# Loading each dense phase's input block in four transfers instead of one

## The chip, the cores and the metric

The kernel runs on one core of a Trainium2 chip. The metric is the time of one execution in microseconds (us), as the device measures it; lower is better. A core has five engines that run side by side, each in the order of its own queue: TensorE (PE; matmuls, with weight loads as PEld), VectorE (DVE), ScalarE (ACT), GpSimd (POOL) and SyncE (SP), which here does nothing but issue transfers between the main memory and the on-chip memory.

## The reference

One layer of a hybrid encoder for a prompt of 2048 tokens and a sample of 32 tokens, in float32, model width 1024, feed-forward width 4096. Cut to what matters:

```python
def trunk_layer(x, mem_k, mem_v, k_past, v_past, shift_prev, wkv0, lw, table):
    z = rmsnorm(x, lw['norm_mix_g']) @ lw['w_in']
    q, k, v, zr = jnp.split(z, ...)
    a_out, k_buf, v_buf = window_attention(q, k, v, k_past, v_past, lw['attn_sink'], table)
    r_out, shift_new, S = rwkv7_mixer(zr, shift_prev, wkv0, lw)        # recurrent over the tokens
    x = x + jnp.concatenate([a_out, r_out], axis=-1) @ lw['w_out']
    x = x + memory_cross_attention(rmsnorm(x, lw['norm_cross_g']), mem_k, mem_v, lw)
    hm = rmsnorm(x, lw['norm_mlp_g'])
    x = x + jnp.square(jax.nn.relu(hm @ lw['w_up'])) @ lw['w_down']
    return x, k_buf, v_buf, shift_new, S
```

The memory's keys and values come from `rmsnorm(mem) @ w_mk` and `rmsnorm(mem) @ w_mv` (256 tokens). A last RMSNorm follows. The outputs are both token blocks and the updated caches and states.

## The kernel before

All activations are kept transposed: 128 rows (partitions) by chunks of the width by tokens. A width of 1024 is eight chunks of 128. The 2080 tokens are worked on in four groups (0 to 3) of 544, 512, 512 and 512 tokens, each in two blocks of 272 or 256.

There are two stages. The first, up to about 1770 us of the trace, holds:

- the dense phases, all made by `prep` (an input block is loaded and split) and `dense` (loop over weight units, and for each over the two blocks): Y and Z (w_in, input x, 8 chunks), M (the memory's keys and values, 8 chunks), O (w_out, input mscr, 8 chunks), C (w_cq, input x2scr, 8 chunks), D (w_co, input cscr, 4 chunks). Z uses the blocks that Y loaded;
- the RWKV tiles R (17 of them, recurrent one after the other, many small matmuls), the window attention tiles A and the cross attention jobs X, and L, which loads blocks for the second stage.

The second stage is the feed-forward part, six blocks of 352 or 320 tokens against 32 weight units up and down, with its own loads.

Float32 accuracy is had from three matmuls for each chunk (`mm3`, lines 230 to 237): the input block is split into a high part xh, rounded by ScalarE, and a low part xl, the rest, by VectorE or GpSimd; weights are split likewise into w_h and w_l (`load_w`, lines 252 to 259: two transfers w_raw of 256 KB for each unit, ScalarE for w_h, then GpSimd or VectorE for w_l). The three products xh w_h, xl w_h and xh w_l are lines 234, 235 and 236. A unit on a block of eight chunks is 24 matmuls that add up in one PSUM tile ps_z, of which there are two; VectorE evacuates it (zo, zoq).

`prep` (lines 264 to 297) loads the block into the tile xb, of which there is one (line 277). Where the phase has a norm (Y, M, C), each chunk gives one xh (ScalarE) and one xl (VectorE), lines 294 to 296, and later, in `rms`, one square on ScalarE, summed on GpSimd, from which the norm comes that the evacuation multiplies by. Where it has none (O, D), each pair of chunks gives one xh and one xl (lines 289 to 292). The next block's load has to wait until the last reader of xb is through. In the listing of the profile, helpers record ScalarE's work at line 66 and VectorE's and GpSimd's at lines 69 and 72.

What sets the order: all of it is written in the order of PLAN (line 35), and a planner at build time then orders each engine's queue from a simulated timeline (line 37), by priorities that the code sets (`setp`, lines 205 to 210): RWKV's serial parts first, the dense matmuls of `mm3` last. At run time each engine follows its queue in order, and a wait holds what stands behind it. Every load of xb, w_raw and the rest stands in SyncE's queue; only a few stores are issued by ScalarE.

The very first block (Y0's first) already comes in four transfers of two chunks (lines 278 to 280, `pe` is true there alone). Y0's second block goes into three tiles of its own (lines 265 to 272).

Of the kernel before, what the change touches and what calls it, by code (L numbers as in the profile page):

```python
# [50 lines left out]
def hymba_step_kernel(  # L51
# [9 lines left out]
    V, G, S, T, Q = nc.vector, nc.gpsimd, nc.scalar, nc.tensor, nc.sync  # L61
# [36 lines left out]
    def pc(key, i, n=1):  # L98
        return par[:, PG[key] + i:PG[key] + i + n]
# [72 lines left out]
    def split(xt, h, l, eng=None):  # L172
        act(h, xt)
        tt(l, xt, h.bitcast(F32), SUB, eng)
# [18 lines left out]
    def rms(pool, xk, n, tag, pe=False, bufs=1):  # L193
        acc, ps = sumsq(pool, xk, n, tag, pe, bufs)
        act(acc, ps, AF.Ln, bias=eps_t, scale=1.0 / D)
        act(acc, acc, AF.Exp, scale=-0.5)
        return acc

    def gsplit(xk, h, l, g):
        act(h, xk, scale=g)  # L200
        stt(l, xk, g, h.bitcast(F32), MUL, SUB)
# [62 lines left out]
    def prep(src, nb, gkey, nk=KC, pe=False, alt=False):  # L264
        if alt:
            xa = [rp.tile([P, 1024], F32, tag=t, name="xa", bufs=BKB if t == "bk" else 1) for t in ("bk", "wa", "lt")]
            xs_ = []
            for j, t in enumerate(xa):
                w = min(3, nk - 3 * j)
                v = t[:, 0:w * nb].rearrange("p (a b) -> p a b", a=w)  # L270
                Q.dma_start(v, src[:, 3 * j:3 * j + w])
                xs_ += [v[:, i] for i in range(w)]

            def xk(k):
                return xs_[k]
        else:
            xb = zp.tile([P, KC, NH], F32, tag="xb", name="xb", bufs=1)
            if pe:
                for k in range(0, nk, 2):
                    Q.dma_start(xb[:, k:k + 2, 0:nb], src[:, k:k + 2])  # L280
            else:
                Q.dma_start(xb[:, 0:nk, 0:nb], src)

            def xk(k):
                return xb[:, k, 0:nb]
        xh = [zp.tile([P, XS, NH], F32R, tag="xh", name="xh", bufs=XB) for k in range(0, nk, XS)]
        xl = [zp.tile([P, XS, NH], F32R, tag="xl", name="xl", bufs=XB) for k in range(0, nk, XS)]
        if gkey is None:
            for k in range(0, nk, 2):
                a, b = divmod(k, XS)  # L290
                split(xb[:, k:k + 2, 0:nb], xh[a][:, b:b + 2, 0:nb], xl[a][:, b:b + 2, 0:nb],
                      ENG[E6] if k % 4 else V)
            return xh, xl, None
        for k in range(nk):
            a, b = divmod(k, XS)
            gsplit(xk(k), xh[a][:, b, 0:nb], xl[a][:, b, 0:nb], pc(gkey, k))
        return xh, xl, lambda: rms(zp, xk, nb, "zt", pe, 3)
# [23 lines left out]
    def zphase(g, units):  # L321
# [3 lines left out]
        if g not in zst:  # L325
            def xprep(b0, nb):
                return prep(xT3[:, :, o + b0:o + b0 + nb], nb, "mix", pe=(g == 0), alt=(g == 0 and b0 > 0))

            zst[g] = ([(lambda b=b: xprep(*b)) if g == 0 and b[0] else xprep(*b) for b in blks], [None] * 2)
# [52 lines left out]
    def memphase():  # L382
        lab("mem")
        xs = [prep(memT.rearrange("(k p) t -> p k t", p=P), NMEM, "mem")]

        def evk(h, bi, b0, nb, ps, r):
            zo = zp.tile([P, NH], F32, tag="zo", name="zok", bufs=3)
            tt(zo[:, 0:nb], ps[:, 0:nb], r, MUL)
            Q.dma_start(kxs[:, h], zo[:, 0:nb])
            Q.dma_start(pmkT[:, h], zo[:, 0:nb])  # L390

        def evv(h, bi, b0, nb, ps, r):
            zo = zp.tile([P, NH], F32, tag="zo", name="zov", bufs=3)
            tt(zo[:, 0:nb], ps[:, 0:nb], r, MUL)
            pt = pmm("pvx")
            for m in range(2):
                T.transpose(pt[:, m * P:(m + 1) * P], zo[:, m * P:(m + 1) * P], ident)
            zv_ = zp.tile([P, NH], F32, tag="zo", name="zovt", bufs=3)
            act(zv_[:, 0:nb], pt[:, 0:nb])
            zv3 = zv_[:, 0:nb].rearrange("p (a b) -> p a b", a=2)  # L400
            Q.dma_start(vxs[:, :, h * P:(h + 1) * P], zv3)
            Q.dma_start(pmv[:, :, h * P:(h + 1) * P], zv3)

        dense(wmk, range(4), xs, [(0, NMEM)], evk)
        dense(wmv, range(4), xs, [(0, NMEM)], evv)

    def ophase(g):
        lab(f"O{g}")
        o, n = GROUPS[g]
        blks = halves_of(g)  # L410
        xs = [prep(mscr[g][:, :, b0:b0 + nb], nb, None) for b0, nb in blks]

        def evac(m, bi, b0, nb, ps, r):
            xr = zp.tile([P, NH], F32, tag="zm", name="xres", bufs=3)
            Q.dma_start(xr[:, 0:nb], xT3[:, m, o + b0:o + b0 + nb])
            zo = zp.tile([P, NH], F32, tag="zo", name="zo2", bufs=3)
            tt(zo[:, 0:nb], ps[:, 0:nb], xr[:, 0:nb], ADD)
            Q.dma_start(x2scr[g][:, m, b0:b0 + nb], zo[:, 0:nb])

        dense(wout, range(8), xs, blks, evac)  # L420
# [507 lines left out]
    for it in PLAN.split():  # L928
        k = it[0]
# [242 lines left out]
```

## Time and profile before

| | |
|---|---|
| median of 3 runs | 3261.2 us (3257.1 to 3262.8) |
| the profiled execution | 3264.6 us |
| its span, first to last instruction | 3262.8 us |
| mean granted TensorE clock | 0.960 |
| loads of xb in one transfer | 31 (23 of eight chunks, 8 of four) |

How to read the rows below: times are us from the start of the span, unless they are marked ns. PE is a matmul, PEld a weight load, SPq a transfer being issued by SyncE. `out<-in` are the program's names of tiles, `x8` a count. In the timeline a row gives the start, the time from there to the end, the engine, the line, the operation, and in brackets how long the engine stood idle before it and what ended that. In the table of stretches PEclk is the granted clock of TensorE as a share of full speed. "DMA to landing" is the time from the start of an issue to the landing of its data.

### The profile page before, as it was taken

What the parts mean: (1) busy time and instruction counts of PE and PEld (TensorE: products, weight loads), DVE (VectorE), ACT (ScalarE), POOL (GpSimd) and SP (SyncE); (2) the same over time, 40 slices, a digit from 0 to 9 for tenths busy, and PEclk for the clock granted to TensorE, in tenths of its full rate; (3) what the DMA queues carried; (4) which work ended last, traced back from release to release, by engine and by line L of the source; (5) the groups of instructions that cost most, each with busy time, mean ns of one, the idle gap of its engine ahead of it and who ended that gap; (6) DMA issues with size and microseconds to landing.
All of it is one profiled execution on the core that took longest, in us unless ns stands there. A gap on an engine that the chain in (4) does not pass through costs nothing.

```text
span 3262.8 us, 64716 instructions
## 1 busy us (share of the span) xinstructions
PE 3037.4 (93%) x25605; PEld 2850.0 (87%) x25605; DVE 1896.0 (58%) x4482; ACT 1247.0 (38%) x2824; POOL 1012.4 (31%) x1017
## 2 busy tenths in 40 slices
PE   8989888998879988898978999999999999999998
PEld 7877776877768977778978999999999999999998
DVE  4588777887777567853334544444445644444446
ACT  5355454444455444445443322222224322222223
POOL 3443354323354343425554410111013511011111
PEclk9989888999989999999989999999999999999999
DMA  5443343334344454446765211111113111111112
GB/s 167 134 115 108 104 130 108 108 96 122 109 122 123 135 150 120 130 129 195 242 214 178 68 51 41 46 46 52 40 46 115 66 44 52 40 52 52 46 46 91
DMA packets 336752, 328.95 MB, mean 101 GB/s; under 512 B 82320, under 2 KB 256064, under 8 KB 336448
## 3 DMA queue, kind: packets, MB, share of 16 engines
q1 hardware_dynamic: 306640, 311.83, 31.0%
q10 hardware_dynamic: 29808, 12.98, 1.6%
q8 instruction: 201, 3.29, 0.4%
q14 instruction: 103, 0.84, 0.1%
HBM read 252.59 MB, written 72.39 MB: 100 GB/s over the span
## 4 chain that ended last, share of the span: by engine, by line
PE 53%; DMA 8%; DVE 7%; ACT 3%; POOL 2%; issue 2%; SPq 1%; DVEq 0%; ACTq 0%; POOLq 0%
PE ps_up L236 7%; PE ps_dn L1002 7%; PE ps_dn L1004 7%; PE ps_dn L1003 7%; PE ps_up L234 7%; PE ps_up L235 7%; PE ps_z L234 2%; PE ps_z L236 2%; PE ps_z L235 2%; DMA xb<-x2scr 2%; DMA lt<-lscr 1%; ACT xh L66 1%; DVE z L69 1%; DVE prd L69 1%; DVE xt L69 1%
## 5 line engine op out<-in xcount | busy, mean ns | idle before, releaser
L234 PE MATMUL ps_z<-xh,w_h 128*128 128x256 f32 (+1 forms) x2368 | 722.8, 305 | 98.3 <-DVE zo L69 41.1
L236 PE MATMUL ps_z<-xh,w_l 128*128 128x256 f32 (+1 forms) x2368 | 715.0, 302 | 0.8 <-POOL w_l L69 0.8
L235 PE MATMUL ps_z<-xl,w_h 128*128 128x256 f32 (+1 forms) x2368 | 714.0, 302 | 1.4 <-DVE xl L72 0.8
L66 ACT ACTIVATE w_h<-w_raw 128x512 fp32r<-128x512 f32 x576 | 344.5, 626 | 777.7 <-PE ps_up L235 258.5
L69 DVE TENSOR_TENSOR x<-ps_dn,x 128x352 f32<-128x352 f32 (+1 forms) x768 | 389.6, 516 | 365.0 <-PE ps_dn L1004 364.5
L234 PEld LDWEIGHTS ps_z<-xh,w_h 128*128 128x128 f32 x2368 | 478.0, 202 | 124.1 <-DVE zo L69 34.2
L69 POOL TENSOR_TENSOR w_l<-w_raw,w_h 128x512 fp32r<-128x512 f32 x300 | 394.9, 1332 | 580.6 <-ACT w_h L66 481.0
L69 POOL TENSOR_TENSOR rl<-rl 128x352 f32<-128x352 f32 (+1 forms) x192 | 161.1, 840 | 1138.4 <-ACT uh L66 1136.4
L1002 PE MATMUL ps_dn<-uh,w_h 128*128 128x352 f32 (+1 forms) x1536 | 492.9, 321 | 4.2 <-DVE x L69 3.1
L236 PE MATMUL ps_up<-fh,w_l 128*128 128x352 f32 (+1 forms) x1536 | 495.4, 323 | 1.2 <-DVE w_l L69 1.2
L1003 PE MATMUL ps_dn<-ul,w_h 128*128 128x352 f32 (+1 forms) x1536 | 491.1, 320 | 5.0 <-DVE ul L69 5.0
L234 PE MATMUL ps_up<-fh,w_h 128*128 128x352 f32 (+1 forms) x1536 | 493.2, 321 | 0.5 <-DVE zo L69 0.5
L235 PEld LDWEIGHTS ps_z<-xl,w_h 128*128 128x128 f32 x2368 | 478.3, 202 | 15.9 <-issue 9.6
L236 PEld LDWEIGHTS ps_z<-xh,w_l 128*128 128x128 f32 x2368 | 478.0, 202 | 15.2 <-issue 10.4
L235 PE MATMUL ps_up<-fl,w_h 128*128 128x352 f32 (+1 forms) x1536 | 491.1, 320 | 0.1
L1004 PE MATMUL ps_dn<-uh,w_l 128*128 128x352 f32 (+1 forms) x1536 | 490.8, 320 | 0.0
L69 DVE TENSOR_TENSOR w_l<-w_raw,w_h 128x512 fp32r<-128x512 f32 x276 | 197.7, 735 | 222.0 <-ACT w_h L66 221.5
L1003 PEld LDWEIGHTS ps_dn<-ul,w_h 128*128 128x128 f32 x1536 | 289.9, 189 | 5.6 <-DVE ul L69 5.3
L1002 PEld LDWEIGHTS ps_dn<-uh,w_h 128*128 128x128 f32 x1536 | 288.6, 188 | 6.5 <-DVE x L69 3.0
L236 PEld LDWEIGHTS ps_up<-fh,w_l 128*128 128x128 f32 x1536 | 288.4, 188 | 1.7 <-DVE w_l L69 1.5
L1004 PEld LDWEIGHTS ps_dn<-uh,w_l 128*128 128x128 f32 x1536 | 289.2, 188 | 0.2
L234 PEld LDWEIGHTS ps_up<-fh,w_h 128*128 128x128 f32 x1536 | 288.3, 188 | 1.3 <-DVE zo L69 0.7
(245 smaller groups left out, 4478.5 us busy)
## 6 DMA issues: line engine op xcount, KB each, us to landing
w_raw<-in_win SPq DMA_DIRECT2D x160, 256.0 KB, 2.9
w_raw<-in_wup SPq DMA_DIRECT2D x136, 256.0 KB, 2.6
w_raw<-in_wdn SPq DMA_DIRECT2D x136, 256.0 KB, 2.6
w_raw<-in_wout SPq DMA_DIRECT2D x64, 256.0 KB, 3.2
zrw<-zo SPq DMA_DIRECT2D x84, 128.0 KB, 2.1
lt<-lscr SPq DMA_DIRECT2D x34, 244.0 KB, 3.8
zin<-zrw SPq DMA_DIRECT2D x16, 512.0 KB, 3.8
w_raw<-in_wcq SPq DMA_DIRECT2D x32, 256.0 KB, 3.4
```

Of the source, the lines that this page charges most:

```text
L66: S.activation(out, in_, func, **kw)
L69: (eng or V).tensor_tensor(out, a, b, op=op)
L234: T.matmul(ps, lhsT=a, rhs=c, start=(k == 0), stop=False)
L235: T.matmul(ps, lhsT=a, rhs=d, start=False, stop=False)
L236: T.matmul(ps, lhsT=b, rhs=c, start=False, stop=(k == nk - 1))
L1002: T.matmul(ps[:, 0:n], lhsT=wh[:, ms], rhs=us[i][0], start=(i == 0), stop=False)
L1003: T.matmul(ps[:, 0:n], lhsT=wh[:, ms], rhs=us[i][1], start=False, stop=False)
L1004: T.matmul(ps[:, 0:n], lhsT=wl[:, ms], rhs=us[i][0], start=False, stop=(i == 1))
```

## The change

In `prep`, the loads of xb that were one transfer of all the block's chunks become one transfer for each two chunks: four for a block of eight chunks, two for a block of four. The tile, its bytes and all that reads it are unchanged.

```diff
@@ -275,11 +275,8 @@
                 return xs_[k]
         else:
             xb = zp.tile([P, KC, NH], F32, tag="xb", name="xb", bufs=1)
-            if pe:
-                for k in range(0, nk, 2):
-                    Q.dma_start(xb[:, k:k + 2, 0:nb], src[:, k:k + 2])
-            else:
-                Q.dma_start(xb[:, 0:nk, 0:nb], src)
+            for k in range(0, nk, 2):
+                Q.dma_start(xb[:, k:k + 2, 0:nb], src[:, k:k + 2])
 
             def xk(k):
                 return xb[:, k, 0:nb]
```

## Rows read from the trace of the kernel before

**Rows 1.** The page, part 1: busy us, share of the span, instructions.

```profile
PE 3037.4 (93%) x25605; PEld 2850.0 (87%) x25605; DVE 1896.0 (58%) x4482; ACT 1247.0 (38%) x2824; POOL 1012.4 (31%) x1017
```

**Rows 2.** Busy us (x instructions) in three stretches; clock, DMA share, GB/s.

```profile
0.00:1420.00 1420.00, 1256.03 (x13757) 1091.45 (x13758) 1029.71 (x2814) 696.34 (x1649) 566.16 (x531) 0.93 0.42 122
1420.00:1770.00 350.00, 307.83 (x2597) 292.94 (x2596) 128.35 (x309) 165.91 (x401) 167.65 (x175) 0.93 0.66 208
1770.00:3262.00 1492.00, 1473.56 (x9257) 1465.66 (x9255) 737.90 (x1360) 384.76 (x774) 278.55 (x311) 1.00 0.17 55
```

**Rows 3.** Chain: shares in 1420 to 1770 us; pieces: start us, us.

```profile
by line: PE ps_z L234 11.5%; PE ps_z L236 10.8%; PE ps_z L235 10.6%; DMA xb<-x2scr 8.8%; issue 6.1%; DMA xres<-x2scr 4.8%; PE xpo L498 4.1%; PE xq L474 3.5%; POOL w_l L69 3.3%; ACT xh L66 3.0%; DMA w_raw<-in_wco 2.8%; DMA x<-x3scr 2.7%; DMA
...
912.35 6.83 DMA xb<-x2scr
...
1739.85 4.57 DMA xb<-cscr
```

**Rows 4.** SyncE on tile xb, whole span: issue ns min/median/max, starts.

```profile
L282 SPq DMA_DIRECT2D xb<-x2scr x8: 524/541/567, 912.3 to 1649.1; - x8
...
  ACT xh L66: 78.8, 24
...
DMA to landing us min/median/max: 2.9/5.6/10.6
```

**Rows 5.** Timeline 1625 to 1638 us: start us, us, engine, line [idle before].

```profile
1626.04 0.52 SPq L282 DMA_DIRECT2D xb<-x2scr  x1
...
1633.76 3.31 ACT L66 ACTIVATE xh<-xb,par 128x256 fp32r<-128x256 f32 x8 [5.21 <-DMA xb<-x2scr]
...
1634.30 0.48 DVE L72 SCALAR_TENSOR_TENSOR xl<-xb,par,xh 128x256 fp32r<-128x256 f32 x1 [5.40 <-ACT xh L66]
1634.70 0.42 DVE L69 TENSOR_TENSOR zo<-ps_z,xres 128x256 f32<-128x256 f32 x1
```

**Rows 6.** Timeline of TensorE: four of the waits near loads of xb.

```profile
919.77 0.59 PE L234 MATMUL ps_z<-xh,w_h 128*128 128x272 f32 x1 [5.44 <-ACT xh L66]
...
1439.84 1.05 PE L225 MATMUL ptm<-td,gs 32*32 32x16 f32 x64 [5.91 <-ACT gs L66]
...
1635.27 0.55 PE L234 MATMUL ps_z<-xh,w_h 128*128 128x256 f32 x1 [3.99 <-DVE zo L69]
...
1745.12 0.80 PE L234 MATMUL ps_z<-xh,w_h 128*128 128x256 f32 x2 [4.39 <-ACT xh L66]
```

**Rows 7.** SyncE on tile xb, 0 to 12 us: the block in four.

```profile
L280 SPq DMA_DIRECT2D xb<-in_xT x4: 399/468/469, 2.9 to 4.3; - x4
...
DMA to landing us min/median/max: 2.9/3.6/4.9
```

**Rows 8.** Timeline 0 to 12 us: SP, then ACT, then PE.

```profile
2.85 1.93 SPq L280 DMA_DIRECT2D xb<-in_xT  x4
4.83 0.94 SPq L257 DMA_DIRECT2D w_raw<-in_win  x2
...
5.88 0.93 ACT L66 ACTIVATE xh<-xb,par 128x272 fp32r<-128x272 f32 x2 [3.86 <-DMA xb<-in_xT]
...
8.49 1.75 ACT L66 ACTIVATE xh<-xb,par 128x272 fp32r<-128x272 f32 x4
...
10.81 0.60 PE L234 MATMUL ps_z<-xh,w_h 128*128 128x272 f32 x1 [10.81 <-ACT w_h L66]
```

**Rows 9.** Timeline 912 to 924 us, VectorE.

```profile
914.88 4.53 DVE L69 TENSOR_TENSOR z<-kk,pp 64x256 f32<-64x256 f32 x4
919.45 1.65 DVE L72 SCALAR_TENSOR_TENSOR km<-wa,par 128x512 f32<-128x512 f32 x1
```

**Rows 10.** Busy us and granted clock around the wait at 914 us.

```profile
905.00:914.00 9.00, 8.43 (x128) 6.99 (x130) 6.85 (x15) 4.91 (x10) 3.33 (x4) 1.00 0.37 106
...
920.00:928.00 8.00, 6.65 (x35) 5.44 (x35) 7.94 (x11) 4.00 (x11) 6.15 (x7) 0.52 0.10 36
```

**Rows 11.** What SyncE's queue waited for: us in total, times, longest.

```profile
SPq L442 <- DMA xb<-x2scr: 5.1, 2, 2.9
```

## The prediction

> **What bounds the kernel now.** First the busy time by engine: TensorE is busy 93% of the span [rows 1]; the reader is to see that no other engine is near. Then the same by stage [rows 2]. From 1770 us on, TensorE is idle for 18 of 1492 us and the granted clock is 1.00. The diff does not touch that stage, and it holds no load of xb. The rest of the idle time is ahead of it: 1420 - 1256 = 164 us up to 1420 us, where the RWKV tiles run among the dense phases, and 350 - 308 = 42 us from 1420 to 1770 us, where mostly dense phases are left. VectorE is busy 73% (1030 of 1420) in the first of these and 37% (128 of 350) in the second. So a shorter wait counts nearly in full in the second, and in the first only where VectorE has nothing else due.
>
> Next the chain of waits. In 1420 to 1770 us the loads of xb from x2scr alone are 8.8% of the chain, 31 us [rows 3]. Over the span I find thirteen xb loads among the chain's long pieces; the first and the last of them are in [rows 3], and together they are 86.4 us. Eleven are of eight chunks (77.7 us; six before 1420 us, five after) and two, of the cscr phases, are of four chunks (4.13 and 4.57 us). The view of tile xb says that a load lands 2.9 to 10.6 us after its issue [rows 4].
>
> Last, one load in order of time [rows 5]. It is issued at 1626.04. ScalarE stands from then until 1633.76, when the whole block has landed, and then makes all eight xh in 3.31 us. VectorE has the first xl ahead of the evacuation of an older result, so that evacuation waits too (1634.70), and TensorE waits 3.99 us for it [rows 6]. One landing holds three queues. Waits of TensorE near such a load from 1420 to 1770 us: six, from 5.91 us (ended 1439.84) to 4.39 us (ended 1745.12) [rows 6], together 26.5 us.
>
> **The change part by part.** There are 31 loads that change: 23 of eight chunks become four transfers, 8 of four chunks become two. The first block of all (Y0) is already loaded in four, and the second one (three tiles of its own) stays. So this trace has the new form once.
>
> *What it shows* [rows 7, 8]: four transfers of 272 KB are issued within 1.93 us, the first at 2.85, and each lands 2.9 to 4.9 us after its own issue. The first xh starts at 5.88, that is 3.03 us after the first issue. The last one is issued at 4.3, and at 2.9 us at the least it cannot have been there before about 7.2: the first xh did not wait for it. The change therefore does what it says; a reader waits for its own transfer, and I give no chance to the opposite. The third pair is being worked on at 8.49, so the pairs are 1.3 us apart ((8.49 - 5.88) / 2), and ScalarE is busy nearly throughout.
>
> *Gain on a load of eight chunks.* Upper bound: its piece of the chain shrinks to 3.03 us. For the eleven: 77.7 - 11 x 3.03 = 44.4 us, or 4.0 each. Lower bound: the last pair lands no sooner than the whole block does now, and up to 1.4 us later since its issue is that much later, but six of the eight xh (6/8 x 3.31 = 2.5 us [rows 5]) are done by then: 2.5 - 1.4 = 1.1 us each, 12 in all. I take the middle, 2.6 each: the first matmul needs only the first pair, but a unit's 24 matmuls need the last. For the two loads of cscr the bounds are 0 (half of the work done earlier, against one more issue) and 1.3 each (4.35 on average less 3.03); I take 0.6.
>
> *Where it is covered.* Before 1420 us the next thing that is late is VectorE. At 914 to 919.77 us TensorE waits 5.44 us for xh [rows 6], but VectorE is at work on RWKV tiles from 914.88 to 919.41 and 919.45 to 921.10 [rows 9], and TensorE's next RWKV matmuls wait for a copy queued behind that. So there I count half: 6 x 2.6 / 2 = 8 us. After 1420 us in full: 5 x 2.6 + 2 x 0.6 = 14 us. If the cover is thinner, the first term is 16; if complete, 0.
>
> *The clock.* Before the wait at 914 us the granted clock is 1.00, which is the level of 2.4 GHz; in 920 to 928 us, after TensorE had stood for 5.44 us, it is 0.52, nearly all at 1.2 GHz [rows 10]. That stretch loses 8 x 0.48 = 3.8 us. Shorter waits should give some of this back. For the six waits of the last stretch the bounds are 0 and 6 x 3.8 = 23 us; waits that shrink from about 4.4 to 2 us may still bring the lower level, so I take 5.
>
> *What it costs.* On SP's queue a load now takes 1.93 us in place of 0.54 [rows 4, 7, 8]: 1.4 more for each of 23, and 0.4 (2 x 0.47 - 0.54, taken as for x2scr) for each of 8, 35 us of SP time. SP mostly waits, and these issues fall behind waits that exist anyway, but what stands right behind a load is late by 1.4 us: the weight halves (w_raw), residual loads, an RWKV tile's zin or lt. Y0 shows it: w_raw is issued at 4.83, right behind the four, and the first matmul at 10.81 waited for w_h, not for xh [rows 8]. Bounds: 0 and 13 x 1.4 = 18 us, if behind each load on the chain something late is queued. I take 8, about six of them. SP also waits at times for the landing of an older transfer that it doesn't need (an xres load stood for xb, 5.1 us in two waits [rows 11]); shorter transfers make that no longer, and I put it at nothing. Bytes are the same, and so are the rows of one chunk, so the transfer itself costs the same on the DMA engines.
>
> A rule that speaks against the change: the Trainium skill, in "DMA: Bandwidth & Descriptors" (Rules for kernel authors), asks for at least 1 MiB per transfer and for many small ones to be made into one, since each pays a fixed part. The rows of Y0 speak against that part being paid one after the other here. By the rule alone the change would only lose; it is the last rival below.
>
> **The sum.** 8 + 14 + 5 - 8 = 19 us less. The profiled execution took 3264.6 us (span 3262.8 and 1.8 around it), so 3245.6; the median of the runs is 3.4 us below the profiled one, so 3242. A measurement of this kernel can tell about 0.2% (6.5 us) from no change.
>
> **The rivals.**
> *Full gain, 3214.* The pieces of the chain shrink to the first pair (44.4 + 2 x 1.3 = 47 us) and the covers and costs cancel. For it: single waits on landing before TensorE's matmuls, and 37% of VectorE after 1420 us. Against it: a unit needs all four pairs, and the last one comes no sooner. Chance 0.15.
> *The gain is hidden, 3258.* The RWKV tiles' own chain and the weights queued behind the loads take all but some 3 us. For it: VectorE's 73%, and only 42 us of TensorE's idle time lie after 1420 us. Against it: a tail in which the loads are on the chain with little beside them. Chance 0.17.
> *TensorE's queue is ordered anew, 3278.* All engines' orders are planned at build time from the planner's idea of when a transfer lands (line 37), by priority. With the first pair due earlier, dense matmuls are put earlier into TensorE's queue, ahead of RWKV's small matmuls, and TensorE, which goes in order, can now stand at each of three more pairs, 1.3 us each, with RWKV's chain behind it. In the 16 loads before 1420 us that is at most 16 x 3 x 1.3 = 62 us; half of it, 31, less the 14 gained later, is 17 slower. It decides from about 11 such waits (14 / 1.3) on. For it: waits of this kind exist now, at 919.77. Against it: TensorE stands there once and long, and one wait is replaced by parts of itself. Chance 0.20.
> *Transfers pay one after the other, 3320.* If the four ran one behind another at the 2.9 us of Y0's shortest, the last pair would come 11.6 us after the first issue in place of 7.1 (77.7 / 11): 4.5 us later, and 13 x 4.5 = 58.5 us more. This is what the skill's rule comes to at its worst. Y0's third pair, in work 5.6 us after the first issue, speaks against it. Chance 0.03.
>
> **How the numbers follow.** The forecast, 3242, has 0.45; its own range is 3228 to 3254, with SP's part at 0 and 6 us more from the clock on one side, and SP's part at 18 and 3 from the clock on the other. Faster by over 0.2% is the forecast and the full gain, 0.60; within 0.2% the hidden gain, 0.17; slower 0.20 + 0.03 = 0.23. The range reaches to 3212 below, the full gain with a little of the clock, and to 3282 above, the reordered queue; what is left out is the serial case and the far ends, under 2 in 10.
>
> **What would show it.** ScalarE's first xh some 3.0 to 3.5 us after the first issue in nearly all phases, and its waits for xb (78.8 us now [rows 4]) under half; TensorE's idle time from 1420 to 1770 us under 30 of the stretch; M's stage unchanged to 2 us; the start of M's stage earlier by about 19 us; a granted clock a little up before 1770 us. The forecast would be wrong if TensorE's idle time before 1420 us grew (the queue rival), if w_h or w_l came to end the waits that xh ends now (SP's part), or if the last pair came over 9 us after the first issue (the serial case).

## The result, and the profile after

The changed kernel takes 3242.0 us (median of four runs, 3235.5 to 3248.4) where the kernel before takes 3260.6: a ratio of 0.9943, with a 95% interval of 0.993 to 0.9956. That is 18.6 us less, and the forecast was 3242. Measured again among the experiments below, it gave 0.995 (0.9932 to 0.9967). The total was right; the terms that it was summed from were not all right, and the experiments show which.

The profiled execution took 3235.5 us, of which the span is 3233.6. The page, part 1, and the same three stages as in [rows 2], with their ends moved to where the stages now end:

```profile
PE 3021.3 (93%) x25605; PEld 2832.1 (88%) x25605; DVE 1897.3 (59%) x4482; ACT 1247.6 (39%) x2824; POOL 1017.8 (31%) x1017
```

```profile
0.00:1400.00 1400.00, 1239.58 (x13758) 1076.78 (x13759) 1019.98 (x2796) 697.52 (x1652) 572.68 (x533) 0.94 0.42 124
1400.00:1740.00 340.00, 308.80 (x2595) 290.38 (x2595) 139.00 (x328) 165.94 (x399) 165.82 (x174) 0.95 0.68 215
1740.00:3233.00 1493.00, 1472.90 (x9253) 1464.94 (x9253) 738.28 (x1360) 384.19 (x774) 279.28 (x312) 1.00 0.17 55
```

The instruction counts of the computing engines are those of before [rows 1]. TensorE's idle time is 160 us up to 1400 us (164 before) and 31 us from there to 1740 us (42 before). The busy time of the first stage is 16.5 us less, at a clock of 0.94 in place of 0.93 [rows 2], and that of the second 1.0 us more. So of the 30 us by which these two stages are shorter in this pair of executions, 15.5 is busy time, for as many instructions, and 14.5 idle time. That must be read with care. The profiled execution of before lies above its median (3264.6 against 3260.6), and that of after below its own (3235.5 against 3242.0). A single pair of profiles can't give the clock's share; the mean over many executions, below, says how little is known of it.

The last stage is unchanged, and begins earlier. TensorE's timeline at its first matmul, before and then after:

```profile
1770.08 0.32 PE L234 MATMUL ps_up<-fh,w_h 128*128 128x352 f32 x1
```

```profile
1739.59 0.32 PE L234 MATMUL ps_up<-fh,w_h 128*128 128x352 f32 x1
```

It lasts 1492.7 us before (3262.8 - 1770.1) and 1494.0 after (3233.6 - 1739.6).

SyncE on tile xb, and who waited for it:

```profile
L279 SPq DMA_DIRECT2D xb<-x2scr x32: 359/460/574, 795.9 to 1624.9; - x32
...
  ACT xh L66: 59.8, 35
...
DMA to landing us min/median/max: 2.7/4.1/7.4
```

Eight issues became 32 of about the same duration, and the median landing came down from 5.6 to 4.1 us [rows 4]. ScalarE's waits fell from 78.8 to 59.8 us only: more of them, and shorter. In the chain of waits, the loads of xb that are among its long pieces were thirteen with 86.4 us together, and are ten with 39.2 us. The shares of 1400 to 1740 us, with the longest piece that is a load of xb and the last one (start us, us):

```profile
by line: PE ps_z L234 9.2%; PE ps_z L235 8.7%; PE ps_z L236 8.6%; DMA xb<-x2scr 6.7%; DMA xres<-x2scr 6.1%; PE xpo L495 5.8%; issue 5.1%; PE xq L471 4.0%; ACT xh L66 3.2%; DMA w_raw<-in_wco 3.2%; DVE xl L72 3.1%; PE xpt L489 2.4%; POOL w_l 
...
1460.03 5.91 DMA xb<-x2scr
...
1708.43 4.68 DMA xb<-cscr
```

The chain lost 47 us of xb and the kernel 18.6: other pieces stand where these stood. In this stretch the loads of xb from x2scr went from 31 us [rows 3] to 23 (6.7% of 340), and the residual's loads (xres) from 17 to 21 us.

One thing in this trace was not foreseen. SyncE's timeline in four short stretches:

```profile
795.86 0.38 SPq L279 DMA_DIRECT2D xb<-x2scr  x1
...
827.11 0.38 SPq L279 DMA_DIRECT2D xb<-x2scr  x1
...
854.69 0.38 SPq L279 DMA_DIRECT2D xb<-x2scr  x1
...
891.62 0.57 SPq L279 DMA_DIRECT2D xb<-x2scr  x1
```

This is one load, the first block of the first cross phase. Whole, it was issued at 912.35 [rows 3], when all of its eight chunks had been written. In pairs, each waits only for its own two chunks, and the planner issues the first of them 117 us earlier. The split is therefore also a change of the plan, and the experiments had to tell the two apart.

### The profile page after: what moved, and what is told of

Same layout as the page of the kernel before. It is cut to its first block, busy times and chain, and to the rows that moved or that the text cites. A ratio compares the mean times of both kernels' runs of the same rounds, so it can differ in the third digit from the quotient of the medians.

```text
span 3233.6 us, 64839 instructions
## 1 busy us (share of the span) xinstructions
PE 3021.3 (93%) x25605; PEld 2832.1 (88%) x25605; DVE 1897.3 (59%) x4482; ACT 1247.6 (39%) x2824; POOL 1017.8 (31%) x1017
## 3 DMA queue, kind: packets, MB, share of 16 engines
q8 instruction: 201, 3.29, 0.4%
## 4 chain that ended last, share of the span: by engine, by line
PE 60%; DVE 15%; DMA 10%; ACT 4%; issue 3%; SPq 1%; POOL 1%; ACTq 0%; DVEq 0%; POOLq 0%
PE ps_up L236 7%; PE ps_dn L999 7%; PE ps_up L235 7%; PE ps_up L234 7%; PE ps_dn L1001 7%; PE ps_dn L1000 7%; PE ps_z L234 3%; PE ps_z L235 3%; PE ps_z L236 3%; DVE z L69 2%; DMA lt<-lscr 2%; DMA lscr<-ab 1%; DVE prd L69 1%; PE pA L225 1%; DVE xt L69 1%
## 5 line engine op out<-in xcount | busy, mean ns | idle before, releaser
L234 PE MATMUL ps_z<-xh,w_h 128*128 128x256 f32 (+1 forms) x2368 | 715.6, 302 | 91.6 <-DVE zo L69 49.9
L236 PE MATMUL ps_z<-xh,w_l 128*128 128x256 f32 (+1 forms) x2368 | 706.0, 299 | 1.1 <-POOL w_l L69 1.1
L234 PEld LDWEIGHTS ps_z<-xh,w_h 128*128 128x128 f32 x2368 | 471.1, 199 | 117.5 <-DVE zo L69 36.4
L235 PEld LDWEIGHTS ps_z<-xl,w_h 128*128 128x128 f32 x2368 | 471.6, 199 | 18.7 <-issue 11.7
L236 PEld LDWEIGHTS ps_z<-xh,w_l 128*128 128x128 f32 x2368 | 470.9, 199 | 13.3 <-issue 7.8
L235 PEld LDWEIGHTS ps_up<-fl,w_h 128*128 128x128 f32 x1536 | 288.5, 188 | 1.4 <-DVE fl L72 1.1
```

What stands on the lines that cost most here:

```text
L234: T.matmul(ps, lhsT=a, rhs=c, start=(k == 0), stop=False)
L235: T.matmul(ps, lhsT=a, rhs=d, start=False, stop=False)
L236: T.matmul(ps, lhsT=b, rhs=c, start=False, stop=(k == nk - 1))
```

## The experiments

They were to tell three theories apart. The first is that the xh of a block start sooner, with its first pair, and run under the rest of the transfer. The second is that the gain, or part of it, comes from what the new plan does, the early issues above all. The third is chance: any new plan moves the time by some 20 us, and this one was lucky. Times are given as ratios to the kernel before, measured beside it, with 95% intervals; a difference in us is the ratio's share of the median of before.

In the kernels that keep the order of before, the planner first orders the program with whole loads; each engine's queue is read off, and the program with split loads is then chained in that order on every engine, with edges that order and do not wait. The transfers of a load stand together where the whole load stood. The queues of all five engines are then those of before, but for the transfers of xb. The traces bear it out: VectorE's 4482 and GpSimd's 1017 instructions follow each other as before.

### All loads in pairs, in the order of before

```diff
+            _step = _chunks(len(_loads), nk)      # 2
+            for k in range(0, nk, _step):
+                Q.dma_start(xb[:, k:k + _step, 0:nb], src[:, k:k + _step])
...
+    for a, b in zip(seq, seq[1:]):                # seq: one engine's queue as before
+        tc.add_manual_dep(have[b], have[a].name, nosync, reason="order")
```

> All 31 loads of xb split as in the change, but every engine's queue is held in the order that the planner gave the kernel before (a load's transfers stand together where the whole load stood). So the pairs land sooner and nothing else changes. Theory 'sooner' (the prediction: what counts is that the first pair lands sooner): 15 to 20 us faster than before, as the change itself. Theory 'order' (each transfer of two chunks depends only on what wrote these two chunks, so the planner can issue it earlier and moves the dense work forward; C0's first pair was issued at 795.9 us in the changed kernel, the whole block at 912.4 before): within 6 us of before. Theory 'chance' (any new plan moves the time by some 20 us either way): within 6 us of before.

Measured: 3242.1 us against 3266.7, **0.9925 (0.9911 to 0.9939)**, 24.5 us less. The split alone, without a new plan, gives all of the gain. SyncE on tile xb, and the stages:

```profile
L281 SPq DMA_DIRECT2D xb<-x2scr x32: 360/462/1529, 898.2 to 1623.4; - x32
...
  ACT xh L66: 32.9, 27
```

```profile
1397.00:1741.50 344.50, 304.17 (x2591) 289.33 (x2590) 132.01 (x306) 167.07 (x401) 167.15 (x175) 0.95 0.67 211
```

ScalarE's waits for xb are 33 us here, 42% of those of before [rows 4]; under the new plan they were 60. Since both kernels run the same queues, the same instruction can be found in both traces, and its shift says where time is gained. ScalarE's stores of lscr, one in each step of the RWKV chain, before:

```profile
435.34 0.61 ACTq L655 DMA_DIRECT2D lscr<-ab  x1
...
945.10 0.62 ACTq L655 DMA_DIRECT2D lscr<-ab  x1
...
1404.40 1.29 ACTq L655 DMA_DIRECT2D lscr<-ab  x2
```

and with the split in the order of before:

```profile
433.88 0.61 ACTq L654 DMA_DIRECT2D lscr<-ab  x1
...
932.42 0.62 ACTq L654 DMA_DIRECT2D lscr<-ab  x1
...
1381.57 1.29 ACTq L654 DMA_DIRECT2D lscr<-ab  x2
```

The shift is 1.5 us at 435, 12.7 at 945 and 22.8 at 1404. The last stage starts at 1742.4 here, 27.7 us earlier. By this pair of traces 23 of the 28 us were gained before 1404 us, where dense phases run beside RWKV tiles, and 5 after it, where the prediction had put most. But such pairs shift without any cause in the code. The kernel of a later section in which one load alone is split has the same order and the same median time as before, and the same store stands 6.6 us earlier in its trace, 9.2 earlier at 665 us. Two executions of the changed kernel itself lie 13.4 us apart there:

```profile
1397.85 1.29 ACTq L653 DMA_DIRECT2D lscr<-ab  x2
...
1385.27 1.29 ACTq L652 DMA_DIRECT2D lscr<-ab  x2
...
1398.70 1.29 ACTq L652 DMA_DIRECT2D lscr<-ab  x2
```

(one load split; the change; the change once more). So the shift only points to a place; the two halves are measured by themselves further on.

What stands in the way in the tail can be read in two blocks. The block that [rows 5] shows, now in pairs (timeline 1597 to 1612 us):

```profile
1598.23 1.92 SPq L281 DMA_DIRECT2D xb<-x2scr  x4
...
1601.52 0.91 ACT L66 ACTIVATE xh<-xb,par 128x256 fp32r<-128x256 f32 x2 [0.33 <-DMA xb<-x2scr]
...
1602.98 0.91 ACT L66 ACTIVATE xh<-xb,par 128x256 fp32r<-128x256 f32 x2 [0.55 <-DMA xb<-x2scr]
...
1605.68 0.42 DVE L69 TENSOR_TENSOR zo<-ps_z,xres 128x256 f32<-128x256 f32 x1 [2.84 <-DMA xres<-x2scr]
...
1611.96 0.36 PE L234 MATMUL ps_z<-xh,w_h 128*128 128x256 f32 x1 [2.63 <-DVE zo L69]
```

The first xh starts 3.29 us after the first issue (7.72 before), as forecast. But the evacuation behind the first xl now waits 2.84 us for its residual. TensorE waits for evacuations twice, 4.98 us together (the second wait, 2.63, is shown), where it waited once for 3.99 [rows 6]. A wait for the block has become a wait for another load. The second block of the second cross phase, whole in the kernel before and then in pairs (timeline 1404 to 1418 us):

```profile
1428.51 0.56 SPq L282 DMA_DIRECT2D xb<-x2scr  x1
...
1434.78 3.31 ACT L66 ACTIVATE xh<-xb,par 128x256 fp32r<-128x256 f32 x8 [4.20 <-DMA xb<-x2scr]
```

```profile
1405.42 1.99 SPq L281 DMA_DIRECT2D xb<-x2scr  x4
...
1407.50 0.89 SPq L257 DMA_DIRECT2D w_raw<-in_wcq  x2
...
1408.37 1.83 ACT L66 ACTIVATE xh<-xb,par 128x256 fp32r<-128x256 f32 x4 [0.88 <-DMA xb<-x2scr]
...
1414.44 0.91 ACT L66 ACTIVATE xh<-xb,par 128x256 fp32r<-128x256 f32 x2 [2.62 <-DMA xb<-x2scr]
...
1417.11 1.05 PE L225 MATMUL ptm<-td,gs 32*32 32x16 f32 x64 [6.27 <-ACT gs L66]
```

The first pair is there after 2.95 us, the last after 9.02, and the whole block of before was there after 6.27. The weights are issued right behind it, and they may share the DMA engines with the last pair; that is not shown. TensorE waits for gs (a tile of RWKV), which ScalarE makes behind the last xh, 6.27 us in place of 5.91 [rows 6].

### More issues, nothing split

```diff
             Q.dma_start(xb[:, 0:nk, 0:nb], src[:, 0:nk])
...
+            for _ in range(nk // 2 - 1):                       # n counts the added transfers
+                Q.dma_start(scr[:, n:n + 1], cst_d[:, n:n + 1])
```

Whole loads in the order of before, each followed on SP's queue by as many transfers of 512 bytes as the split adds; nobody reads them. It measures what SP's queue pays.

> Whole loads and all queues in the order of before, but behind each of the 31 loads stand as many more transfers (three, or one for four chunks) of 512 bytes into a tile that nobody reads. They cost SyncE the issue and almost nothing else. By the prediction's term: 8 us slower than before, bounds 0 and 18. If SyncE's time doesn't matter: within 3 us.

Measured: 3266.3 us, **0.9999 (0.9986 to 1.0013)**, 0 +- 4 us. SyncE on the added tile:

```profile
L286 SPq DMA_DIRECT2D scr<-in_cst x77: 422/612/1757, 32.7 to 1741.9; - x77
```

The 77 issues are there, of 0.61 us each, some 47 us on SP's queue, and the end doesn't move. SP's part of the sum was 8, and it is nothing.

### The change with the last pair issued first

```diff
-            for k in range(0, nk, 2):
-                Q.dma_start(xb[:, k:k + 2, 0:nb], src[:, k:k + 2])
+            qs = [Q.dma_start(xb[:, k:k + 2, 0:nb], src[:, k:k + 2]) for k in range(0, nk, 2)]
+            if not pe:
+                for a, b in zip(qs[-1:] + qs[:-2], qs[:-1]):
+                    tc.add_manual_dep(b.ins, a.ins.name, nosync, reason="last pair first")
```

No pair can now leave before the last one, so the early issues at 796 to 892 us are gone. The first pair is still issued right behind it. (`pe` marks the very first block, which was in four before.)

> As the change, newly planned, but of each load's transfers the last pair is issued first, and the others behind it in SyncE's queue. Where the chunks are written in order (x2scr), no transfer can now be issued before the whole block is there; the first pair lands about 0.5 us later than in the change. 'Sooner': 14 to 18 us faster than before, nearly as the change. 'Order': at most 8 us faster, most of the gain is gone. 'Chance': anything within 20 us.

Measured: 3248.2 us, **0.9948 (0.9935 to 0.9962)**, as much as the change itself. This kernel has a plan of its own too, so it is not the change less the early issues and nothing else; but without them the gain is all there. ScalarE's waits for xb are 76.8 us here, nearly those of before: under a new plan, these waits don't rank the kernels.

### Only the cross phases split

```diff
+            step = 2 if pe or gkey == "cross" else nk
-            for k in range(0, nk, 2):
+            for k in range(0, nk, step):
```

> Only the eight loads from x2scr (phases C) are split, newly planned. 'Sooner': eight of 31 loads, and of the 86.4 us of such loads on the chain of before some 43: half the gain, 7 to 11 us faster. 'Order': only here are the chunks written one by one, so nearly the whole gain, 14 to 20 us faster. 'Chance': anything within 20 us.

Measured: 3258.2 us, **0.9978 (0.9965 to 0.999)**, some 7 us (3 to 11). These are the loads that the chain showed most of in the tail (over the span they are seven of its thirteen long pieces, 49.3 of the 86.4 us, not some 43), and they give a little under half of what the change gives, under a plan of their own.

### The early loads alone, and the late ones alone

In the order of before, the first has pairs up to load 16 (the last to start before 1400 us), the second from load 17 on (seven of eight chunks, eight of four).

```diff
+    return 2 if i < 17 else nk                    # early
...
+    return 2 if i == 0 or i >= 17 else nk         # late
```

> Queues in the order of before; of the 31 loads only the 16 that are issued before 1420 us are split. The prediction's sum: VectorE covers half there, 8 us faster (bounds 0 and 16). The shift of RWKV's steps in the trace with all loads split under the same order says otherwise: 23 us earlier by 1405 us, so 19 to 24 us faster.

> Queues in the order of before; only the 15 loads that are issued after 1420 us (seven of eight chunks, eight of four) are split. The prediction's sum: 14 us faster, with the clock up to 19. By the shift in the trace with all loads split: 3 to 8 us faster.

Measured: early **0.9965 (0.9952 to 0.9978)**, 11.4 us (7 to 16); late **0.9982 (0.9968 to 0.9996)**, 5.9 us (1 to 10). The forecast had it the other way round, 8 and 14. The 19 to 24 us that the shift of the RWKV steps had promised for the early loads lie above the interval: the pair of traces had overstated them. The early loads give 6 us more than the late ones (2 to 10, from the two sets of executions). Together they give 17, which the width of the intervals doesn't tell from the 24.5 of all loads in the same order.

### Two transfers instead of four: two and six chunks, six and two

```diff
+    cuts = [0, 2, nk] if nk == 8 else [0, 2, 4]   # two_six
...
+    cuts = [0, 6, nk] if nk == 8 else [0, 2, 4]   # six_two
```

In the first the first pair comes soon and the rest late, in the second the work on six chunks lies under the transfer of two.

> Queues in the order of before; loads of eight chunks come as two chunks and then six, loads of four as two and two. If what counts is that the first pair lands sooner (the upper bound of the prediction's gain): nearly all of the 24 us of four pairs, 18 to 24 us faster. If what counts is that the work on the early chunks lies under the transfer of the rest (its lower bound): a third of it (two chunks of the six that pairs put ahead), 6 to 10 us faster.

> Queues in the order of before; loads of eight chunks come as six chunks and then two, loads of four as two and two. First pair sooner: the first chunks come little sooner than in one load, 3 to 8 us faster. Work under the transfer: all but the last two chunks are done when the last pair lands, if the six land well before it, 12 to 20 us faster.

Measured: **0.9958 (0.9941 to 0.9975)**, 13.7 us, and **0.9957 (0.9941 to 0.9972)**, 14.0 us. ScalarE's timeline at the second block of the second cross phase, first issued at 1420.30 and at 1416.16:

```profile
1423.49 0.91 ACT L66 ACTIVATE xh<-xb,par 128x256 fp32r<-128x256 f32 x2 [1.12 <-DMA xb<-x2scr]
...
1427.55 2.50 ACT L66 ACTIVATE xh<-xb,par 128x256 fp32r<-128x256 f32 x6 [3.15 <-DMA xb<-x2scr]
```

```profile
1421.75 3.30 ACT L66 ACTIVATE xh<-xb,par 128x256 fp32r<-128x256 f32 x8 [3.75 <-DMA xb<-x2scr]
```

The kernels do what they were made for here: first xh after 3.2 us but the last one done after 9.8 in the one, 5.6 and 8.9 in the other. Each gives about half of the gain. The 9 to 19 us of six and two lie above the 3 to 8 expected if only the sooner first chunks counted, so the work under the transfer counts. The 8 to 19 us of two and six reach into both of its expectations. That the prediction's two bounds for a load, the sooner first pair and the work under the transfer, are two parts of about equal size fits these runs but is not shown: both kernels cut the loads of four chunks in pairs as well, each has a little of the other's part, and at this block pairs (2.95 and 9.93 us) are no better than two and six.

### The change once more, and one load split alone

The first is the change itself. The second is the change with every load whole but that of the memory block (`gkey == "mem"` in the condition above), planned anew, to see what a new plan alone does.

> The changed kernel itself, beside the others on one chip. If the new plan adds nothing to the split (the split under the order of before gave 24 us): 19 to 25 us faster than before. If the new plan takes something back: 14 to 19 us faster.

> Newly planned, but only the one load of the memory's block is split. Its own worth by the trace of before is at most 3 us. If a new plan alone moves the time by chance: anything up to 20 us either way. If not: 0 to 3 us faster.

Measured: **0.995 (0.9932 to 0.9967)** and **1.0001 (0.9988 to 1.0015)**. The change repeats, and splitting one load alone moves nothing. But that kernel's trace has the order of before on every queue (VectorE's 4482, GpSimd's 1017 and SyncE's other transfers one for one): the planner made no new plan, so this run doesn't test what a new plan does by chance. What speaks against chance is that three different orders with all loads in pairs, that of before, that of the change and that with the last pair first, are all faster by 16 to 24.5 us. The change (16 and 19 us) and the split in the order of before (24.5) come near each other; whether the new plan takes some back, these intervals don't settle.

### Four and four chunks, and one chunk in each transfer

Both in the order of before (`min(nk, 4)` and 1 as the step).

> Queues in the order of before; loads of eight chunks come as four and four, loads of four chunks in one. If the gain goes with the number of pieces: between two_six or six_two (14 us) and whole loads, about 10 to 16 us faster. If two pieces do all that matters: 20 to 24 us.

> Queues in the order of before; one transfer for each chunk, so eight or four for a load. If smaller pieces go on helping: 27 to 32 us faster. If the last piece's landing is what is left (it came 9.0 us after the first issue in C1's second block, against 6.25 for the whole block): 18 to 26 us, as with pairs. If issuing costs now: under 18 us.

Measured: two transfers of four chunks **0.9936 (0.9919 to 0.9953)**, 21 us; eight of one chunk **0.9968 (0.9955 to 0.9982)**, 10.4 us. In the first the whole tile of a load of four chunks stays in one transfer. ScalarE at the same block, first issued at 1406.14:

```profile
1409.97 3.31 ACT L66 ACTIVATE xh<-xb,par 128x256 fp32r<-128x256 f32 x8 [1.76 <-DMA xb<-x2scr]
```

First xh after 3.8 us and the last one done after 7.1 (6.3 and 9.6 whole): at this block one cut in the middle has most of both parts. The second was expected to be at least as good as pairs, and is not. SyncE on tile xb in it:

```profile
  ACT xh L66: 25.7, 29
...
DMA to landing us min/median/max: 2.0/3.0/10.6
```

Its waits for xb are the smallest of all, and its transfers land soonest. By the shifts of the RWKV steps it goes from 3.5 us ahead of before at 514 us to 2.4 behind at 1195, where pairs go from 3.4 to 15.4 ahead. That doesn't show where it loses: its profiled execution was the slowest of its twelve (3263.1 us at a median of 3252.9, clock 0.960), and the kernel with the late loads alone, whose loads in that stretch are whole, goes from 1.3 ahead to 4.3 behind. Why it gains less is open. SP's issues are dearer in it (185 more in place of 77), and the run with 77 tiny transfers doesn't exclude that more than twice as many cost something.

## Why the prediction was right, point by point

- **What bounds the kernel, and that the split does what it says**: right. With every queue as before, the split alone gave 24.5 us. In that kernel the first xh for which ScalarE waited started 3.0 to 4.1 us after the first issue for blocks from in_xT and x2scr, a little above the 3.0 to 3.5 that was named; for some blocks of the O and D phases (mscr, cscr) it was up to 5.9. One reading of [rows 5] was wrong: ScalarE did not stand all the time from 1626.04 to 1633.76, for it made a w_h at 1627.91, and its wait was 5.21 us; no term of the sum uses it.
- **Gain of one load, between 1.1 and 4.0, taken as 2.6**: the work under the transfer counts, by the run with six and two chunks; the sooner first pair fits the run with two and six (14 us each, of 24.5) and isn't shown by itself. All loads together were put at 8 + 14, and 24.5 or 17 were measured, by the one run or by the two halves. That single chunks, which land soonest, gave 10 doesn't follow from these two mechanisms and stays open.
- **The late loads, 14, and the clock, 5**: mis-sized. Measured 5.9 (1 to 10), with what the clock gives included. The step that failed is "After 1420 us in full". A low share of VectorE was taken to mean that nothing else was late there. In the two blocks read, the next late things were other transfers: a residual, and the last pair itself, with weights issued behind it. The stretch had 42 us of idle time, as one rival said.
- **The early loads, 8 with bounds 0 and 16**: measured 11.4 (7 to 16), inside the bounds. Whether VectorE covers less than the half that was taken, or the ten early loads that are not on the chain give the rest, no run tells apart.
- **The clock by itself**: 5 was taken for a gain between 0 and 23. The mean granted clock of all executions rose from 0.9640 to 0.9648 with the split in the order of before, and from 0.9645 to 0.9665 with the change. Over the span that is an estimate of 2.6 and 6.5 us (0.0008 x 3242, 0.0020 x 3248), around the size taken, but the means are known no better than that (to 0.0013 and 0.0019 at 95%). With the early loads alone it fell, from 0.9654 to 0.9636, and the kernel was 11.4 us faster all the same. So no run shows the clock's term; what there is of it counts within the gains above, not beside them.
- **SyncE's queue, 8 with bounds 0 and 18**: mis-sized; 0 +- 4. That SP's waits hide these issues is likely and not shown (in that run SP stood 1145 us for VectorE's w_l alone). The first matmul of [rows 8], given as a case of weights that are late behind four transfers, is none: ScalarE made w_h right behind its last xh, without a wait for w_raw (the next row of that timeline, before):

```profile
10.15 1.13 ACT L66 ACTIVATE w_h<-w_raw 128x512 fp32r<-128x512 f32 x2
```

  In the trace after, w_h and w_l did not come to end the waits that xh ended, apart from one wait of 2.9 us in the tail.
- **The sum** is therefore right by luck, through errors against each other: its gains came to 27 (8, 14 and 5) where the two halves gave 17 with the clock's part in it, and its cost of 8 was nothing.
- **Full gain, 3214**: the chain lost the 47 us that this rival names, and the time did not follow. **Hidden, 3258**: true of most of the tail, not of what lies ahead of it. **TensorE's queue ordered anew, 3278**: the order did change, and in the trace after the steps of RWKV run up to 13 us later than before at 1004 us, but they are 19 ahead at 1404 (25 later and 6 ahead in the second execution), and TensorE's idle time before it did not grow. **Serial transfers, 3320**: fell, though one last pair did come 9.0 us after its first issue, which the prediction named as its sign.
- **Its own signs**: the last stage ("M's stage" there) unchanged to 2 us, right (1.3). Its start 19 us earlier: 30 in the profiled pair and 13 in the second execution, so the executions' scatter is a large part. The clock a little up ahead of it: 0.94 and 0.95 for 0.93, right in this pair. TensorE's idle time in the tail under 30: 31. ScalarE's waits for xb under half: wrong for the change (76%), right for the split in the order of before (42%).
- **The rule of the Trainium skill** ("DMA: Bandwidth & Descriptors", Rules for kernel authors: for the most bandwidth, at least 1 MiB per transfer) was set against the change. The runs do not bear it out for this use, in which the aim is not bandwidth: 1 MiB in four transfers of 256 KB gave 24.5 us, in two of 512 KB 21 us, in eight of 128 KB still 10 us. Readers of a whole block had waited until all of it had landed.

## What to carry to other kernels

When one landing holds a queue that works chunk by chunk, cut the transfer where its reader can start; one cut in the middle brought most of it here (21 of 24.5 us) and eight pieces brought less than four. Don't size the gain by the chain's pieces: ask for each which other load or evacuation is due next, since VectorE's busy share of 37% said nothing of transfers that are late. When a change also lets a planner order anew, force the old order once: it tells the edit from the plan. And see in the trace that a kernel made to have a new plan has one.

## What of the hardware was not expected

- SP's queue took 77 more transfers, 47 us of issue, at no cost to the end that shows (0.9999, 0.9986 to 1.0013).
- The last of four transfers can land later than the whole block did (the xh that waits for it starts 9.0 against 6.3 us after the first issue) although the bytes are the same; in another block the whole sequence kept ScalarE in work with waits of 0.3 to 0.6 us.
- Eight transfers of one chunk landed soonest (median 3.0 us against 4.3 for pairs) and had ScalarE wait least for xb (25.7 us against 32.9), and gave less than half of the gain. Why is open.
